# An encoder layer's output projection with two sets of places for its weights, the first half of its norm formed in the projection's own pass, and up products of two units around the last tile

## The chip, the core and the metric

The kernel runs on one core of one Trainium2 chip. TensorE multiplies matrices, VectorE and ScalarE work element by element, GpSimd (POOL) here mostly issues DMAs, and SyncE (SP) issues most of the others. The metric is the device time in microseconds (us) from launch to end; the time before is the median of three runs.

## The reference

One layer of a streaming encoder, for 1024 prompt frames and 64 sample frames of width 1024:

```python
merged = sigmoid(ga) * ya + sigmoid(gb) * yb
x = x + merged @ w_out                      # output projection, 1024 x 1024
n = x * rsqrt(mean(x * x) + 1e-6) * g_ffn
x = x + (silu(n @ w_ff1) * (n @ w_ff3)) @ w_ff2      # 1024 -> 2816 -> 1024
y = x * rsqrt(mean(x * x) + 1e-6) * g_final
```

What comes ahead of `merged` (a norm, one large input projection, a gated convolution, banded attention with its caches) is not touched. All is computed in float32.

## The kernel before

**Products of float32.** `split` writes a tensor as a high half (a ScalarE copy, CAST in the rows) and a low half (a VectorE subtraction of that copy). A product of two such tensors is three TensorE products: high x high, high x low, low x high. So nearly every operand costs one ScalarE and one VectorE operation before TensorE may use it, and the low half waits for the high half.

**Order.** The code is written straight down; a scheduler then fixes the order on each engine, and each engine works strictly through its own list. Pools (`tile_pool`) hold a number of places for each tag, and a new tile waits until the last user of its place is done.

**The merge** (`mgp`, names `ga`, `gb`, `ya`, `yb`) makes `merged` in eight rounds of 128 channels, each in three slices of the frames. It leaves it split, with channels on the partitions: `mg`, four tiles by channel half and frame half, and `ms` for the 64 sample frames. Its last product is on `yb`.

**Output projection.** Nine tiles of frames: 0 to 7 are prompt frames, tile 8 the sample frames. The result's 1024 columns are made in two passes of 512, in the order `ORDER` = 8, 0, 4, 1, 5, 2, 6, 3, 7. `wo_half(hf)` loads the weights of a pass (`wor`, two DMAs of 1 MB) and splits them into eight pairs `woh`, `wol` in a pool with eight places for each, so the second pass takes the places of the first. `token_product` issues 24 products for a prompt tile, 16 for tile 8 (`wo`); `residual` adds `x` on VectorE (for tile 8 after a ScalarE copy `fold`); the result goes to DRAM (`x1_d`).

**Second pass and norm.** `second(i)` loads the tile's first half back, adds the second half's result, forms the sum of squares over 1024 columns on ScalarE (line 891), the factor by `rstd_of` (square root on ScalarE, small VectorE rows, lines 228 to 234) and the normalised row `xg` by one VectorE operation over 1024 columns (line 893). `turned(i, xg)` transposes `xg` with eight TensorE operations into `xt`. For tiles 0 to 3 `first_half` splits `xt` into `mg` (reused as operands) and copies it to `sums`; for tiles 4 to 7, `second_half` forms sums and differences with the tile's partner in `sums` and splits them into `tt` 6, 7, 5 and the other `mg`.

**Up projection.** Frames and channels are halved, and each 2 x 2 block product is made with seven products, the steps `STEPS` = 1, 2, 6, 7, 5, 4, 3. A `Unit` is 256 columns of `w_ff1` (a0, a1, ...) or `w_ff3` (b0, b1, ...); the order is a0, b0, a1, b1 and so on. `prep(step)` splits the unit's weights (`wha`, `wla` for a, `whb`, `wlb` for b) from its raw load (`rawa`, `rawb`). Steps 1, 6, 5, 3 add up in PSUM tile A, 2 in B, 7 and 4 in D, so `Aa<-mg` is step 1 of a0, `Ba<-mg` step 2, `Aa<-tt` step 6 or 5, `Ab<-mg`, `Bb<-mg` steps 1 and 2 of b0. The first two steps read only `mg` of the first frame half. `run(unit, done, ahead, between)` issues all seven and prepares the next unit; for a0, `rest_of_x` is called after step 2 and turns the last tile (7):

```python
    def rest_of_x(si):
        ...
        if si == 1:
            turned(*last)
            wp_stack.close()
            hp = ctx.enter_context(tc.tile_pool(name="hp", bufs=2, reuse_waits="tile"))
            for st in range(2, len(STEPS)):
                unit.prep(st)
```

The down projection follows and is not touched.

Of the kernel before, what the change touches and what calls it, by code (L numbers as in the profile page):

```python
# [79 lines left out]
def encoder_kernel(ctx: ExitStack, tc: tile.TileContext, ins, outs):  # L80
# [717 lines left out]
    tt = {p: tpool.tile([P, 2, 4, HT], F32R, tag=f"o{p}", name=f"tt{p}") for p in (6, 7, 5)}  # L798
# [9 lines left out]

    def wo_half(hf):
        r = []  # L810
        for kq in range(2):
            raw = rpool.tile([P, 4, 512], F32, tag="raw", name=f"wor{hf}_{kq}")
            nc.sync.dma_start(
                raw,
                ins["w_out"][0][kq * 512 : (kq + 1) * 512, hf * 512 : (hf + 1) * 512].rearrange(
                    "(k p) n -> p k n", p=P
                ),
            )
            for k in range(4):
                hi = ws.tile([P, 512], F32R, tag="wh", name=f"woh{hf}_{kq}_{k}")  # L820
                lo = ws.tile([P, 512], F32R, tag="wl", name=f"wol{hf}_{kq}_{k}")
                split(hi, lo, raw[:, k])
                r.append((hi, lo))
        return r
# [602 lines left out]
```

## Time and profile before

| | us |
|---|---|
| three runs: median (lowest, highest) | 1553.8 (1553.78, 1555.74) |
| profiled execution, span from first to last instruction | 1555.5 |
| TensorE busy | 1511.3 |
| first pass of the projection, from the merge's last product on | 52.35 |
| second pass | 54.69 |
| from there to the end of step 2 of b0 | 44.69 |

For the profiled execution no time of its own stands beside its span; the highest of the runs is 0.2 above it. Rows read: start, duration, engine, line, operation, result<-operands, partitions x elements; in square brackets the idle time of the engine before it and what ended that. In the table by stage PEclk is the granted TensorE clock as a share of full speed. Matmuls overlap, so the distance of their starts, not their duration, is their price.

### The profile page before, as it was taken

Reading aid. Unit: us, or ns where it says so; the run is one execution under the profiler, and the core shown is the slowest. Engines: PE = TensorE matmul, PEld = TensorE weight load, DVE = VectorE, ACT = ScalarE, POOL = GpSimd, SP = SyncE. Lnnn points to the kernel's source line nnn. Section 1 sums busy time; section 2 is a strip of 40 time slices with the busy share of each in tenths; the row PEclk is TensorE's granted clock in tenths of the full one; section 3 lists DMA queues with packets and bytes.
Section 4 is the critical chain, followed back from the end, with each engine's and each line's share of the span. In section 5 each row is a group of like instructions: output and inputs, shape, how many; then the busy total and the mean of one; then the engine's idle time right before and its main releaser. Section 6 shows DMA issues by size and latency. Waiting matters only on the chain.

```text
span 1555.5 us, 24418 instructions
## 1 busy us (share of the span) xinstructions
PE 1511.3 (97%) x9407; PEld 1419.1 (91%) x9407; DVE 930.3 (60%) x1877; ACT 622.9 (40%) x1234; POOL 77.5 (5%) x146
## 2 busy tenths in 40 slices
PE   7998999999999999999997999999999999999997
PEld 6888999999999999998886999999999998788886
DVE  7524665555553435664388666666666667757577
ACT  7423454444442132442255444444444444512123
POOL 0110000000000000000100100000101111000000
PEclk9999999999999999999997999999999999999999
DMA  8688785444421323554331443334434338777685
GB/s 280 199 235 232 185 253 145 136 136 127 134 86 41 55 72 42 157 163 154 128 125 50 144 147 126 123 124 143 153 139 153 140 138 295 246 234 240 210 264 202
DMA packets 168661, 247.18 MB, mean 159 GB/s; under 512 B 17025, under 2 KB 117265, under 8 KB 168545
## 3 DMA queue, kind: packets, MB, share of 16 engines
q1 hardware_dynamic: 152400, 191.47, 40.6%
q0 software_dynamic: 14992, 52.05, 8.9%
q10 hardware_dynamic: 1152, 2.10, 0.4%
q8 instruction: 74, 1.21, 0.3%
q14 instruction: 43, 0.34, 0.1%
HBM read 161.91 MB, written 85.23 MB: 159 GB/s over the span
## 4 chain that ended last, share of the span: by engine, by line
PE 60%; issue 29%; DMA 4%; POOL 3%; DVE 3%; ACT 1%; SPq 0%; POOLq 0%; ACTq 0%; DVEq 0%
PE A L1349 7%; PE p L183 6%; PE p L184 6%; PE p L185 6%; PE D L1349 3%; POOL h_d L1100 2%; PE B L1349 2%; PE t L589 2%; PE pv L614 2%; PE Ab L1033 1%; PE ys L1237 1%; PE Aa L1033 1%; PE pvv L414 1%; PE pvv L412 1%; PE s L559 1%
## 5 line engine op out<-in xcount | busy, mean ns | idle before, releaser
L183 PE MATMUL p<-xn,whi 128*128 128x384 f32 (+1 forms) x576 | 193.2, 336 | 0.0
L184 PE MATMUL p<-xn,whi 128*128 128x384 f32 (+1 forms) x576 | 189.8, 330 | 0.0
L185 PE MATMUL p<-xn,wlo 128*128 128x384 f32 (+1 forms) x576 | 189.8, 329 | 0.0
L1349 PE MATMUL A<-ring,ht 128*128 128x512 f32 x528 | 127.7, 396 | 3.9 <-ACT acc L1359 3.8
L1349 PEld LDWEIGHTS A<-ring,ht 128*128 128x128 f32 x528 | 99.6, 190 | 27.2 <-ACT acc L1359 5.0
L183 PEld LDWEIGHTS p<-xn,whi 128*128 128x128 f32 x576 | 109.1, 189 | 1.4 <-DVE kst L131 0.3
L184 PEld LDWEIGHTS p<-xn,whi 128*128 128x128 f32 x576 | 109.2, 190 | 0.1
L185 PEld LDWEIGHTS p<-xn,wlo 128*128 128x128 f32 x576 | 108.9, 189 | 0.0
L522 DVE CUSTOM_DVE_ANT_0 p<-s,bias 128x640 f32<-128x640 f32 (+5 forms) x72 | 47.8, 664 | 98.2 <-PE s L560 98.1
L130 ACT CAST ring<-w2r 128x512 fp32r<-128x512 f32 (+1 forms) x78 | 43.6, 588 | 104.4 <-PE A L1349 50.8
L130 ACT CAST hq<-sa 128x512 fp32r<-128x512 f32 x77 | 47.7, 619 | 92.0 <-DVE sa L1112 58.1
L130 ACT CAST whi<-raw 128x1024 fp32r<-128x1024 f32 x44 | 46.0, 1050 | 92.5 <-PE ch L184 42.6
L131 DVE TENSOR_TENSOR hq<-sa,hq 128x512 fp32r<-128x512 f32 x77 | 53.1, 690 | 38.6 <-ACT hq L130 38.5
L131 DVE TENSOR_TENSOR wlo<-raw,whi 128x1024 fp32r<-128x1024 f32 x44 | 53.7, 1221 | 24.5 <-ACT whi L130 24.4
L1033 PE MATMUL Aa<-mg,wha 128*128 128x272 f32 x352 | 61.0, 295 | 3.9 <-ACT mg L130 3.2
L131 DVE TENSOR_TENSOR wla<-rawa,wha 128x512 fp32r<-128x512 f32 x55 | 37.8, 688 | 44.0 <-ACT wha L130 44.0
L1349 PE MATMUL D<-ring,ht 128*128 128x512 f32 x264 | 63.5, 392 | 0.0
L1100 POOL DMA_DIRECT2D h_d<-hq x77 | 41.0, 533 | 431.2 <-DVE hs L131 213.6
L1033 PE MATMUL Aa<-tt,wha 128*128 128x272 f32 x352 | 59.7, 291 | 2.2 <-ACT tt L130 2.2
L1349 PEld LDWEIGHTS D<-ring,ht 128*128 128x128 f32 x264 | 49.9, 189 | 11.1
L1033 PE MATMUL Ab<-mg,whb 128*128 128x272 f32 x352 | 58.3, 288 | 0.0
L1033 PE MATMUL Ab<-tt,whb 128*128 128x272 f32 x352 | 58.2, 287 | 0.0
(308 smaller groups left out, 3898.3 us busy)
## 6 DMA issues: line engine op xcount, KB each, us to landing
h_d<-hq POOLq DMA_DIRECT2D x77, 512.0 KB, 3.4
ht<-h_d SPq DMA_DIRECT2D x154, 256.0 KB, 3.5
raw<-in_w_in SPq DMA_DIRECT2D x18, 1024.0 KB, 5.7
rawa<-in_w_ff SPq DMA_DIRECT2D x11, 1024.0 KB, 5.7
rawb<-in_w_ff SPq DMA_DIRECT2D x11, 1024.0 KB, 5.4
w2r<-in_w_ff SPq DMA_DIRECT2D x11, 1024.0 KB, 6.0
qd<-q_d SPq DMA_DIRECT2D x32, 272.0 KB, 4.3
x<-in_x_prompt SPq DMA_DIRECT2D x8, 512.0 KB, 3.9
```

Source lines behind the costliest of these rows:

```text
L130: act.copy(hi, src)
L131: vec.tensor_tensor(lo, src, hi.bitcast(F32), op=ALU.subtract)
L183: mm(out, a, p, start=k == 0, stop=False)
L184: mm(out, a, q, start=False, stop=False)
L185: mm(out, b, p, start=False, stop=k == kt - 1)
L412: mm(pv[:n], a, wvh[:, k, :], start=k == 0, stop=False)
L522: vec.tensor_tensor_reduce(out=s if len(ps.shape) == 2 else s.rearrange("p (a b) -> p a b", a=2), in0=ps, in1=bias if len(ps.shape) == 2 e ...
L589: nc.tensor.transpose(tp[:, i * P : (i + 1) * P], s[:, i * P : (i + 1) * P], ident)
L614: mm(pv[:, :, lo:hi], v[:, kb, :], pt[:, :, kb - base, lo:hi], start=i == 0, stop=i == len(blocks) - 1,)
L1033: mm(t[:, j, :HN], x[:, k, :], moving(p, l, k, j * HN, HN), start=p in (1, 2, 7) and k == 0 and n == 0, stop=k == 3 and n == 2, skip_group ...
L1100: nc.gpsimd.dma_start(h_d[p, c - 1], hq.rearrange("p i l t -> p (i l t)").bitcast(F32))
L1349: mm(t, ht[k][:, j, x], w[:, l], start=p in (1, 2, 7) and k == 0 and n == 0, stop=k == len(ks) - 1 and n == 2, skip_group_check=p in (6, 5 ...
```

## The change

The first pass gets its own places for its weights: `wo_hi` (a pool on the side) is copied during the merge's last rounds, `wo_lo` is formed after the merge in the space that `tt` 7 takes later; the second pass's weights are split during the first pass. The first pass runs in the order 0 to 8 and forms, for each tile, the first half of the sum of squares (`more`) and the first half times the gain row, which goes to DRAM (`y0_d`) and comes back as the first half of `xg` in pass two. There ScalarE scales the first half and VectorE the second. `norm_factor` is moved up, and its factor of -2 is met by a gain row scaled by -0.5. `first_half` copies in two parts, and `sums` has four slots for five. Units a0 and b0 are started by hand: steps 1 and 2 of a0, the last tile's transposes (in PSUM places of their own), steps 1 and 2 of b0, and then the rest of a0. The weight sum `s1` moves from preparation step 2 to 3.

```diff
+    def wo_load(hf):
+        ...
+            raw = rpool.tile([P, 4, 512], F32, tag="raw", name=f"wor{hf}_{kq}")
+            nc.sync.dma_start(raw, ...)
     with tc.tile_pool(name="mgp", bufs=3, reuse_waits="tile") as mp:
...
+                if m == 7:
+                    wo_raw = wo_load(0)
+                    wo_hi = t6pool.tile([P, 8, 512], F32R, tag="o6", name="wo_hi")
+                    for k in range(8):
+                        act.copy(wo_hi[:, k], wo_raw[k // 4][:, k % 4])
...
+        act.activation(gb_row, gb_row, AF.Copy, scale=-0.5)
+        for k in range(8):
+            vec.tensor_tensor(wo_lo[:, k], wo_raw[k // 4][:, k % 4], wo_hi[:, k].bitcast(F32), op=ALU.subtract)
+        w2_raw = wo_load(1)
-        for i in ORDER:
+        for i in range(9):
...
-            token_product(ps, i, mg_rows(i), KD, lambda k: w[k])
+            token_product(ps, i, mg_rows(i), KD, lambda k: (wo_hi[:, k], wo_lo[:, k]))
             residual(i, ps, xt, 512, f"o0_{i}")
             nc.gpsimd.dma_start(x1_d[t0 : t0 + n, :512], xt[:n])
+            act.activation(sq[:n, :512], xt[:n], AF.Square, accum_out=ssq0[:n, i : i + 1])
+            vec.tensor_scalar(more[:n, i : i + 1], ssq0[:n, i : i + 1], 1.0 / D, EPS, op0=ALU.mult, op1=ALU.add)
+            y0 = wp.tile([P, D], F32, tag="xg", name=f"y0_{i}")[:, :512]
+            vec.tensor_tensor(y0[:n], xt[:n], gb_row[:n, :512], op=ALU.mult)
+            nc.gpsimd.dma_start(y0_d[t0 : t0 + n], y0[:n])
+            if i < 8:
+                w2_prep(i)
         def second(i):
-            xt = wp.tile([P, D], F32, tag="x1", name=f"x1_{i}")
-            nc.sync.dma_start(xt[:n, 512:], x_rows(i)[:, 512:])
-            nc.sync.dma_start(xt[:n, :512], x1_d[t0 : t0 + n, :512])
+            nc.sync.dma_start(xg[:n, :512], y0_d[t0 : t0 + n])
+            nc.sync.dma_start(xt[:n], x_rows(i)[:, 512:])
...
-            act.activation(xg[:n], xt[:n], AF.Square, accum_out=ssq[:n])
-            r = rstd_of(wp, ssq[:n], n, f"f{i}")
-            vec.scalar_tensor_tensor(xg[:n], xt[:n], r[:n], gb_row[:n], op0=ALU.mult, op1=ALU.mult)
+            act.activation(sq[:n, :512], xt[:n], AF.Square, accum_out=ssq[:n])
+            r = norm_factor(wp, ssq[:n], n, f"f{i}", more[:, i : i + 1])
+            act.activation(xg[:n, :512], xg[:n, :512], AF.Copy, scale=r[:n])
+            vec.scalar_tensor_tensor(xg[:n, 512:], xt[:n], r[:n], gb_row[:n, 512:], op0=ALU.mult, op1=ALU.mult)
...
+    sa_step(0)
+    sa_step(1)
+    turned(*last)
+    wp_stack.close()
+    hp = ctx.enter_context(tc.tile_pool(name="hp", bufs=2, reuse_waits="tile"))
+    for si in range(2, len(STEPS)):
+        ua.prep(si)
+    sb_step(0)
+    sb_step(1)
+    for si in range(2, len(STEPS)):
+        sa_step(si)
+        ub.prep(si)
```

Line numbers shift: 891, 893, 903, 927, 1033 and 1100 become 929, 932, 949, 973, 1080 and 1131. Names carry numbers of their own in the order below (`wo0_8`: pass one, tile 8; the last number only counts tiles).

TensorE at the start of the first pass, before:

```order
L836 MATMUL wo0_8_7464<-woh0_0_0_7428,ms_6436 128x512 [waits DVE_49,Activation_49]
L832 MATMUL wo0_0_7488<-woh0_0_0_7428,mg00_6429 128x512 [waits DVE_49]
L837 MATMUL wo0_8_7464<-wol0_0_0_7429,ms_6436 128x512 [waits DVE_49]
L836 MATMUL wo0_8_7464<-woh0_0_1_7432,ms_6436 128x512 [waits Activation_49]
L833 MATMUL wo0_0_7488<-wol0_0_0_7429,mg00_6429 128x512
L837 MATMUL wo0_8_7464<-wol0_0_1_7433,ms_6436 128x512 [waits DVE_49]
L836 MATMUL wo0_8_7464<-woh0_0_2_7436,ms_6436 128x512 [waits Activation_49]
L834 MATMUL wo0_0_7488<-woh0_0_0_7428,mg00_6429 128x512
```

and now:

```order
L837 MATMUL wo0_0_7459<-wo_hi_7295,mg00_6430 128x512 [waits DVE_49]
L837 MATMUL wo0_1_7497<-wo_hi_7295,mg00_6430 128x512 [waits DVE_49]
L838 MATMUL wo0_0_7459<-wo_lo_7435,mg00_6430 128x512 [waits DVE_49]
L839 MATMUL wo0_0_7459<-wo_hi_7295,mg00_6430 128x512
L837 MATMUL wo0_0_7459<-wo_hi_7295,mg00_6430 128x512
L838 MATMUL wo0_1_7497<-wo_lo_7435,mg00_6430 128x512
L839 MATMUL wo0_1_7497<-wo_hi_7295,mg00_6430 128x512
L838 MATMUL wo0_0_7459<-wo_lo_7435,mg00_6430 128x512 [waits DVE_49]
```

Tile 0 stands first where tile 8 stood, no high half is waited for, and only the low halves (`wo_lo`, on VectorE) are.

VectorE around the last tiles, the rows from the residual of tile 3 to its normalised second half, now (before there were 23 rows from the residual to `xg_3`, with all of tile 6's norm among them):

```order
L855 TENSOR_TENSOR x_3_8229<-wo_3_8231,x_3_8229 128x512
L973 TENSOR_TENSOR sums_8220<-xt_6_8272,sums_8220 128x512
L869 TENSOR_SCALAR nvf_8260<-ssq_3_8258,more 128x1
L973 TENSOR_TENSOR sums_8220<-xt_6_8272,sums_8220 128x512
L871 RECIPROCAL nyf_8262<-nsf_8261 128x1
L132 TENSOR_TENSOR wla_1_8362<-rawa_8357,wha_1_8361 128x512
L872 SCALAR_TENSOR_TENSOR nzf_8263<-nyf_8262,nvf_8260 128x1
L973 TENSOR_TENSOR sums_8220<-sums_8220 128x512
L873 SCALAR_TENSOR_TENSOR nrf_8264<-nzf_8263,nyf_8262 128x1
L132 TENSOR_TENSOR tt_7792<-sums_8220,tt_7792 128x4x128
L932 SCALAR_TENSOR_TENSOR xg_3_8227<-x_3_8229,nrf_8264,gb_row 128x512
```

These are the rows that the transposes of tile 3 wait for. VectorE further down, the last rows up to the low half of `mg` from tile 3's transposes, which step 1 of a0 waits for, before:

```order
L927 TENSOR_TENSOR sums_8185<-sums_8185 128x512 x2
L131 TENSOR_TENSOR mg_6432<-xt_6_8237,mg_6432 128x4x128
L131 TENSOR_TENSOR tt_7419<-sums_8185,tt_7419 128x4x128
L131 TENSOR_TENSOR mg_6431<-sums_8185,mg_6431 128x4x128
L850 TENSOR_TENSOR x_7_8260<-wo_7_8263,x_7_8260 128x512
L131 TENSOR_TENSOR wla_6_8423<-sf,wha_6_8422 128x512
L131 TENSOR_TENSOR wla_7_8428<-rawa_8322,wha_7_8427 128x512
L131 TENSOR_TENSOR wla_5_8432<-sf,wha_5_8431 128x512
L228 TENSOR_SCALAR v_f_8293<-ssq_7_8291 128x1
L131 TENSOR_TENSOR wla_4_8436<-rawa_8322,wha_4_8435 128x512
L230 RECIPROCAL y_f_8295<-s_f_8294 128x1
L131 TENSOR_TENSOR mg_6429<-xt_3_8306,mg_6429 128x4x128
```

and now:

```order
L132 TENSOR_TENSOR tt_7790<-sums_8220,tt_7790 128x4x128
L973 TENSOR_TENSOR sums_8220<-sums_8220 128x512
L132 TENSOR_TENSOR mg_6433<-xt_6_8272,mg_6433 128x4x128
L855 TENSOR_TENSOR x_7_8297<-wo_7_8299,x_7_8297 128x512
L132 TENSOR_TENSOR mg_6432<-sums_8220,mg_6432 128x4x128
L132 TENSOR_TENSOR wla_2_8366<-rawa_8357,wha_2_8365 128x512
L869 TENSOR_SCALAR nvf_8328<-ssq_7_8326,more 128x1
L132 TENSOR_TENSOR wlb_1_8370<-rawb_8359,whb_1_8369 128x512
L871 RECIPROCAL nyf_8330<-nsf_8329 128x1
L132 TENSOR_TENSOR wlb_2_8374<-rawb_8359,whb_2_8373 128x512
L872 SCALAR_TENSOR_TENSOR nzf_8331<-nyf_8330,nvf_8328 128x1
L132 TENSOR_TENSOR mg_6430<-xt_3_8340,mg_6430 128x4x128
```

From tile 3's residual to that low half VectorE has 37 operations before (23 over 512 or more columns a partition) and 24 now (17 of them so).

TensorE around the transposes of the last tile, before:

```order
L1033 MATMUL Ba0_8366<-mg10_6430,wha0_2_8328 128x272 x4
L1033 MATMUL Ba0_8366<-mg10_6430,wla0_2_8329 128x272 x2
L903 MATMUL xt2_7_8394<-ident_69,xg2_7_8290 128x128 x8
L1033 MATMUL Aa0_8335<-tt6_7418,wha0_6_8422 128x272
L1033 MATMUL Da0_8480<-tt7_7419,wha0_7_8427 128x272
L1033 MATMUL Aa0_8335<-tt6_7418,wha0_6_8422 128x272 x2
L1033 MATMUL Da0_8480<-tt7_7419,wha0_7_8427 128x272 x2
L1033 MATMUL Aa0_8335<-tt6_7418,wha0_6_8422 128x272
L1033 MATMUL Aa0_8335<-tt6_7418,wla0_6_8423 128x272 x2
```

and now, with what follows up to the first product that reads `tt`:

```order
L1080 MATMUL Ba0_8404<-mg10_6431,wha0_2_8365 128x272 x4
L1080 MATMUL Ba0_8404<-mg10_6431,wla0_2_8366 128x272 x2
L949 MATMUL xt2_7_0_8432<-ident_69,xg2_7_8295 128x128 x4
L949 MATMUL xt2_7_1_8433<-ident_69,xg2_7_8295 128x128 x4
L1080 MATMUL Ab0_8484<-mg00_6430,whb0_1_8369 128x272 x4
L1080 MATMUL Ab0_8484<-mg00_6430,wlb0_1_8370 128x272 x2
...
L1080 MATMUL Bb0_8511<-mg10_6431,whb0_2_8373 128x272 x4
L1080 MATMUL Bb0_8511<-mg10_6431,wlb0_2_8374 128x272 x2
...
L1080 MATMUL Aa0_8377<-tt6_7792,wha0_6_8462 128x272 x4
```

Two steps of b0, 48 products, stand between the transposes and the first product on `tt` 6, where there was nothing. In pass two each tile's transposes now stand directly ahead of a product group; before they stood up to 18 products into one.

More of the change, by code (lines that the diff above doesn't have):

```diff
@@ L763, in encoder_kernel @@
     ms = mspool.tile([P, KD, 2, TS], F32R, tag="ms", name="ms")
+    t6pool = ctx.enter_context(tc.tile_pool(name="t6pool", bufs=1, reuse_waits="tile", side="right"))
+    wo_raw = []
+    def wo_load(hf):
+        r = []
+        for kq in range(2):
+            raw = rpool.tile([P, 4, 512], F32, tag="raw", name=f"wor{hf}_{kq}")
+            nc.sync.dma_start(
+                raw,
+                ins["w_out"][0][kq * 512 : (kq + 1) * 512, hf * 512 : (hf + 1) * 512].rearrange(
+                    "(k p) n -> p k n", p=P
+                ),
+            )
+            r.append(raw)
+        return r
     with tc.tile_pool(name="mgp", bufs=3, reuse_waits="tile") as mp:
@@ L796, in encoder_kernel @@
     hp0 = ctx.enter_context(tc.tile_pool(name="hp0", bufs=1, reuse_waits="tile"))
[L798 removed]
+    wo_lo = tpool.tile([P, 8, 512], F32R, tag="o7", name="wo_lo")
     ax = mg.t
@@ L807, in column @@
         return i * P if i < 4 else HT + (i - 4) * P
[L809 to L824, printed above, removed]
     def token_product(ps, i, x, kt, w, first=True, last=True):
@@ L898, in turned @@
             n = TT[i][1]
-            pt = bank2("A", f"xt2_{i}").rearrange("p a (b t) -> p a b t", t=P)
+            if i == ORDER[-1]:
+                pt = [
+                    psA.tile([P, 512], F32, tag="mm", name=f"xt2_{i}_{hf}").rearrange("p (b t) -> p b t", t=P)
+                    for hf in range(2)
+                ]
+            else:
+                two = bank2("A", f"xt2_{i}").rearrange("p a (b t) -> p a b t", t=P)
+                pt = [two[:, 0], two[:, 1]]
             for hf in range(2):
@@ L1009, in prep, with runner @@
                 self.plain(3, a12)
-    def run(unit, done, ahead, between=None):
+    def runner(unit, done):
         nm = unit.nm
@@ L1022, in shot, with step @@
             snap[key] = s
-        for si, p in enumerate(STEPS):
+        def step(si):
+            p = STEPS[si]
             key = {1: "A", 6: "A", 5: "A", 3: "A", 2: "B", 7: "D", 4: "D"}[p]
@@ L1052, in run @@
                 done(0, 1, src, None)
-            if between:
-                between(si)
-            for u in ahead:
-                u.prep(si)
-    nxt_unit = Unit(ins["w_ff1"][0][:, : 2 * P], "a0")
-    nxt_unit.prep(0)
-    nxt_unit.prep(1)
-    hp = None
-    def rest_of_x(si):
-        nonlocal hp
-        if si == 1:
-            turned(*last)
-            wp_stack.close()
-            hp = ctx.enter_context(tc.tile_pool(name="hp", bufs=2, reuse_waits="tile"))
-            for st in range(2, len(STEPS)):
-                unit.prep(st)
+        return step
+    hp = None
     names = [(l, p) for p in range(NF // 2) for l in "ab"]
@@ L1256, in encoder_kernel @@
             refill()
-        run(unit, (gate_done if l == "a" else hidden_done)(p), ahead, rest_of_x if n == 0 else None)
+        step = sb_step if n == 1 else step_of(n, unit)
+        for si in range(len(STEPS)):
+            if n > 1 or si > 1:
+                step(si)
+            for u in ahead:
+                u.prep(si)
+        unit = nxt_unit
     up_stack.close()
```

93 lines of the change are left out of this document (58 added, 35 removed).

## Prediction

> **What bounds the kernel now.** First the page's busy shares: TensorE works 97% of the span, so only a stretch in which it stands still or runs at a lower clock can give time back.
>
> ```profile
> PE 1511.3 (97%) x9407; PEld 1419.1 (91%) x9407; DVE 930.3 (60%) x1877; ACT 622.9 (40%) x1234; POOL 77.5 (5%) x146
> PEclk9999999999999999999997999999999999999999
> ```
>
> The one dip of the granted clock inside the span is in the slice from 817 to 856, the end of the output projection. So second, a table by stage: the projection's first pass, its second pass, the join to the up products (to the end of the second step of unit b0), and what follows.
>
> ```profile
> core 0: us, PE busy (x) PEld busy (x) DVE busy (x) ACT busy (x) POOL busy (x), PEclk, DMA share, GB/s
> 713.70:766.05 52.35, 50.14 (x208) 40.23 (x209) 16.65 (x27) 9.53 (x18) 4.37 (x8) 0.97 0.44 146
> 766.05:820.74 54.69, 54.69 (x266) 44.43 (x264) 43.60 (x108) 30.53 (x63) 4.88 (x9) 1.00 0.42 144
> 820.74:865.43 44.69, 35.61 (x232) 34.03 (x232) 31.43 (x56) 20.17 (x35) 0.54 (x1) 0.81 0.18 58
> 865.43:905.00 39.57, 38.93 (x312) 38.71 (x311) 26.68 (x45) 17.27 (x33) 4.29 (x8) 1.00 0.40 146
> ```
>
> Pass two and the stage after it are full; the loss is at the start of pass one and in the join. Third, TensorE's timeline there.
>
> ```profile
> 713.39 0.31 PE L185 MATMUL yb<-ob,wlo 128*128 128x320 f32 x1
> 715.91 0.50 PE L836 MATMUL wo<-woh,ms 128*128 128x512 f32 x1 [2.21 <-ACT woh L130]
> ...
> 760.49 0.40 PE L832 MATMUL wo<-woh,mg 128*128 128x512 f32 x1
> 766.05 0.39 PE L836 MATMUL wo<-woh,ms 128*128 128x512 f32 x1
> 769.69 0.39 PE L832 MATMUL wo<-woh,mg 128*128 128x512 f32 x1
> ...
> 820.50 0.29 PE L1033 MATMUL Ba<-mg,wha 128*128 128x272 f32 x1
> 823.55 1.94 PE L903 MATMUL xt<-ident,xg 128*128 128x128 f32 x8 [2.77 <-DVE xg L893]
> 829.69 0.82 PE L1033 MATMUL Aa<-mg,wha 128*128 128x272 f32 x2 [3.16 <-ACT mg L130]
> 830.79 0.59 PE L1033 MATMUL Aa<-mg,wha 128*128 128x272 f32 x1 [0.28 <-DVE mg L131]
> ...
> 842.51 0.52 PE L1033 MATMUL Aa<-tt,wha 128*128 128x272 f32 x2 [2.18 <-ACT tt L130]
> 843.24 0.82 PE L1033 MATMUL Da<-tt,wha 128*128 128x272 f32 x2 [0.21 <-ACT tt L130]
> ...
> 862.42 0.66 PE L1033 MATMUL Bb<-mg,whb 128*128 128x272 f32 x4
> 865.43 0.66 PE L1033 MATMUL Ab<-tt,whb 128*128 128x272 f32 x4
> ```
>
> A tile of 24 products takes 766.05 - 760.49 = 5.56 us (0.232 each), the sample tile's 16 take 3.64, a step of an up unit 865.43 - 862.42 = 3.01. Pass one is worth 8 x 5.56 + 3.64 = 48.1 and takes 52.35: 4.2 lost. The join is worth nine steps (27.1) and two groups of transposes (0.94 each, below), 29.0, and takes 44.69: 15.7 lost. Each gap drags a slow clock behind it, but not always:
>
> ```profile
> 716.95:720.40 3.45, 3.45 (x10) 2.64 (x9) 3.45 (x7) 2.54 (x5) 0.00 (x0) 0.51 0.87 226
> 822.85:836.20 13.35, 8.73 (x35) 7.76 (x36) 12.45 (x26) 5.77 (x11) 0.54 (x1) 0.50 0.21 67
> 843.40:846.80 3.40, 3.40 (x16) 3.35 (x17) 2.83 (x5) 0.89 (x2) 0.00 (x0) 0.53 0.00 0
> 1104.30:1108.00 3.70, 3.70 (x31) 3.70 (x31) 2.89 (x5) 2.21 (x5) 0.53 (x1) 1.00 0.54 217
> ...
> 1103.14 0.78 PE L1033 MATMUL Da<-tt,wha 128*128 128x272 f32 x4 [2.19 <-DVE sa L1087]
> 890.21 0.78 PE L1033 MATMUL Da<-tt,wha 128*128 128x272 f32 x4 [0.64 <-DVE sa L1087]
> ```
>
> Gaps of 2.21 and 2.18 us were followed by some 3.4 us at half clock, one of 2.19 by none.
>
> **The change, part by part.** VectorE and ScalarE rows that carry the terms:
>
> ```profile
> 713.74 0.49 DVE L781 TENSOR_TENSOR gb<-yb,gb 128x320 f32<-128x320 f32 x1 [0.94 <-PE yb L185]
> 715.88 4.91 DVE L131 TENSOR_TENSOR wol<-wor,woh 128x512 fp32r<-128x512 f32 x8
> 715.24 4.25 ACT L130 CAST woh<-wor 128x512 fp32r<-128x512 f32 x8
> 814.05 0.69 DVE L850 TENSOR_TENSOR x<-wo,x 128x512 f32<-128x512 f32 x1 [1.36 <-PE wo L834]
> 822.12 1.28 DVE L893 SCALAR_TENSOR_TENSOR xg<-x,r_f,gb_row 128x1024 f32<-128x1024 f32 x1
> 830.07 0.67 DVE L131 TENSOR_TENSOR mg<-xt,mg 128x512 fp32r<-128x512 f32 x1
> L893 DVE SCALAR_TENSOR_TENSOR xg<-x,r_f,gb_row 128x1024 f32<-128x1024 f32 x6 | 7.7, 1283 | 0.2
> L891 ACT ACTIVATE xg<-x 128x1024 f32<-128x1024 f32 x7 | 7.4, 1059 | 2.1 <-DVE x L850 2.1
> ```
>
> In a row, a 128x512 operation takes (4.91 - 0.69) / 7 = 0.60 on VectorE and (4.25 - 0.62) / 7 = 0.52 on ScalarE.
>
> *Start of pass one.* The eight copies of the weights' high halves move into the merge: 4.25 us on ScalarE, spread over its last 40 us, where it is not the limit (row below). The two loads keep their places in SP's queue. Tile 0 comes first, whose merged rows are done a third of a round early. The low halves stay behind the last merge product: the first follows the multiply of 713.74, starts near 714.2, ends near 714.9. TensorE has two products before that (to 714.2), so 0.7 us of gap remains. The other seven low halves come every 0.60, with about 1.1 for the merge's last slice between, and end near 720.0; the 27 products that TensorE has by then need 27 x 0.232 = 6.3 us, to 721.2, so it sets the pace. Gain 4.2 - 0.7 = 3.5. Ends: 1.8 if the slow clock comes after all (3.45 us at half cost 1.7), 4.2 if nothing is left. I take 3.4; the gap of 0.64 at 890 kept the full clock.
>
> ```profile
> 680.00:714.00 34.00, 33.70 (x206) 33.43 (x204) 19.49 (x42) 12.95 (x31) 0.00 (x0) 1.00 0.37 112
> x_d<-xr POOLq DMA_DIRECT2D x8, 256.0 KB, 2.6
> x<-x_d SPq DMA_DIRECT2D x8, 256.0 KB, 3.0
> ```
>
> *Rest of pass one.* Per tile VectorE gains a product with the gain row (0.69), one split (0.69) and a small row, beside the residual (0.69): 2.2 of 5.56 us. ScalarE gains a square over 512 (estimate 0.6, half of 1059 ns and a fixed part) and a copy (0.62). Cost 0; the cover is the tile's 5.56 us. The second weights no longer wait for free places, which cost nothing before either (766.05 follows without a gap).
>
> *Round trip of y0.* POOL issues nine more stores; SP's nine reloads of x1 become nine of y0. The tight one is the sample tile, last in pass one and first in pass two. After its last product: copy, two adds and the product with the gain row, 0.2 + 0.6 + 3 x 0.69 = 2.9; the store (behind another, 0.5) lands 2.6 later, the reload 3.0 after that, a scale of 0.6: 9.6 us. TensorE needs it after 3.64 + 5.56 + 10 x 0.232 = 11.5. Cost 0, slack 1.9; if the slack is gone, the price is the excess, once, since SP holds the next reloads only that long.
>
> *Pass two.* Its 54.69 are 48.1 of products and seven groups of transposes, 0.94 each. Both stay. But before, a tile's transposes stand as late as 18 products into the next tile but one; now each group stands ahead of the next product, so a tile's chain from residual to normalised row must fit into 0.94 + 5.56 = 6.5 us. For tile 3, VectorE has seven large rows and four small ones up to its last: 7 x 0.60 + 4 x 0.15 = 4.8, or 5.2 with the ScalarE steps waited for. For tile 1, the fullest, it has eight large and four small, 5.4, and some 0.5 where a low half waits for ScalarE's copy: 5.9. It fits by 0.6. Cost 0; ends -0.8 (split waits inside the old groups) and three such tiles 1.5 late, +4.5.
>
> *Join, first gap.* Before, TensorE ran freely at 830.79, 10.05 after pass two. What ends last is the low half of tile 3's first block (830.07). From that tile's residual to there VectorE works through 23 large rows, two of them 1.28 long, and 14 small: 23 x 0.60 + 2 x 0.6 + 14 x 0.1 = 16.4, measured 830.74 - 814.05 = 16.7. Now it is 17 large and 7 small: 17 x 0.60 + 7 x 0.13 = 11.1, with 0.4 of waits 11.5. The residual starts 0.2 after its product and that ends 6.5 before pass two does, so the end is 5.2 to 5.4 after pass two. Gain 10.05 - 5.4 = 4.7. Ends 3 and 6. The slow clock after it I leave as it was (830.79 to 836.20).
>
> *Join, second gap.* After tile 7's transposes TensorE now has two steps of unit b0, 6.0 us. VectorE needs eight large rows for the first sum that the next step reads: 4.8, with waits 5.3. So the gap of 2.18 + 0.21 goes, and the half clock behind it (3.40 x 0.47 = 1.6): gain 4.0. If that cover failed, what is late next is the second sum, 0.6 behind.
>
> Sum: 3.4 + 0 + 4.7 + 4.0 = 12.1 us, which makes the span 1543.4 from 1555.5. The span is 1.7 above the median of the runs (1553.8), 0.2 under the highest; I take the 12.1 from the median: 1541.7.
>
> The remaining first gap is about 3 us, with a product or two in it. The Trainium skill, page "TensorE: Matmul & The Clock Gate", section "Why this matters for your kernels", warns only of idle gaps above about 3 us. By that rule the restart would keep the full clock, and the sum would be that of rival 3 below. The row of 2.21 with clock 0.51 behind it does not agree with the rule, the row of 2.19 with 1.00 behind it does.
>
> **The rivals.** (1) *Transposes late.* Three of the tiles whose chain shares VectorE with a second-half tile miss the 6.5 us by 1.5: for it speaks the margin of 0.6, against it that VectorE's work per pair falls. 12.1 - 4.5 = 7.6: 1546.2. (2) *No gain at the start*: the low halves alone keep TensorE waiting, and the clock drops as at 716.95; 8.7 remains: 1545.1. (3) *No slow clock in the join*: the 5.4 us at half clock from 830.79 to 836.20 cost 2.7, so 12.1 + 2.7 = 14.8: 1539.0. The gap at 1103.14 speaks for it, the clock from 823 to 836 against. (4) *Slower*: the transposes ahead of the products turn every tile's chain into a wait. If the chain stays as long as tile 3's was (814.05 to 823.40, 9.4 us), seven tiles pay 9.4 - 6.5 = 2.9 each, 20.3 in all: 12.1 - 20.3 = 8.2 slower, 1562.0. It decides from a chain of 6.5 + 12.1 / 7 = 8.2 us on. Against it: the shorter list of rows above. (5) *Nothing*: a chain of about 8.2 us, or the join's gain lost to later waits on the same VectorE queue; the full stage after 865.43 speaks against it.
>
> **How the numbers follow.** Forecast 0.61 (own range 1539.5 to 1544.5), rival 1 0.13, 2 0.08, 3 0.07, 4 0.06, 5 0.05. Faster by over 0.2% (3.1 us, about what a measurement of this kernel can tell from no change): 0.61 + 0.13 + 0.08 + 0.07 = 0.89; within it 0.05; slower 0.06. The range takes the first four cases: low 1553.8 - (4.2 + 4.7 + 4.0 + 2.7) - 1 for a shorter first gap, about 1537.0; high 1546.2 and the 1.7 of a slow clock at the start, about 1548.0. What lies outside is 4 and 5 and a little more.
>
> **What would show it.** In the new trace: a gap under 1 us ahead of the first projection product and a clock of 1.00 behind it (pass one near 49 us); pass two still near 54.7 with no wait ahead of transposes; the first up product running freely some 5.4 us after pass two; no gap after tile 7's transposes; that join near 36 us. The forecast is wrong if transposes wait tile by tile, or if the first gap stays near 10 us because ScalarE's copy of tile 3 comes later than VectorE's list says.

## The result and the profile after

The changed kernel takes 1543.5 us (median of 4 runs, 1542.41 to 1545.24), the kernel before 1553.8 (4 runs), ratio 0.9931 with a 95% interval of 0.9917 to 0.9945. The forecast was 1541.7, range 1537.0 to 1548.0. The changed kernel's profiled execution took 1543.16 us, its span 1541.4. Its page, busy shares and granted clock:

```profile
PE 1503.1 (98%) x9407; PEld 1413.3 (92%) x9407; DVE 930.4 (60%) x1877; ACT 630.5 (41%) x1267; POOL 82.3 (5%) x155
PEclk9999999999999999999999999999999999999999
```

TensorE's busy time fell by 8.2 us with the same 9407 instructions: part of the gain is clock, and the dip is gone from the row. The table by stage, cut as before (columns as in its header):

```profile
core 0: us, PE busy (x) PEld busy (x) DVE busy (x) ACT busy (x) POOL busy (x), PEclk, DMA share, GB/s
714.26:763.55 49.29, 48.57 (x210) 39.05 (x209) 23.20 (x44) 11.65 (x27) 8.69 (x16) 1.00 0.66 230
763.55:817.92 54.37, 54.37 (x265) 44.54 (x264) 42.09 (x98) 33.45 (x76) 5.41 (x10) 1.00 0.37 118
817.92:852.32 34.40, 31.14 (x233) 30.53 (x232) 29.15 (x52) 19.67 (x38) 1.08 (x2) 0.95 0.25 84
```

Pass one is 3.1 shorter, pass two as long as it was, the join 10.3 shorter. TensorE's timeline at the same places:

```profile
714.11 0.31 PE L186 MATMUL yb<-ob,wlo 128*128 128x320 f32 x1
714.26 0.62 PE L837 MATMUL wo<-wo_hi,mg 128*128 128x512 f32 x2
715.60 0.50 PE L838 MATMUL wo<-wo_lo,mg 128*128 128x512 f32 x1 [0.72 <-DVE wo_lo L888]
...
817.69 0.40 PE L839 MATMUL wo<-woh,mg 128*128 128x512 f32 x1
817.93 1.04 PE L949 MATMUL xt<-ident,xg 128*128 128x128 f32 x8
818.72 0.37 PE L1080 MATMUL Ba<-mg,wha 128*128 128x272 f32 x1
819.36 0.36 PE L1080 MATMUL Aa<-mg,wha 128*128 128x272 f32 x1 [0.28 <-DVE mg L132]
822.03 0.52 PE L1080 MATMUL Aa<-mg,wha 128*128 128x272 f32 x2 [2.31 <-ACT mg L131]
823.23 0.40 PE L1080 MATMUL Aa<-mg,wha 128*128 128x272 f32 x1 [0.68 <-DVE mg L132]
...
830.39 1.03 PE L949 MATMUL xt<-ident,xg 128*128 128x128 f32 x8
831.18 0.75 PE L1080 MATMUL Ab<-mg,whb 128*128 128x272 f32 x4
```

The start's gap is 0.72 instead of 2.21. The transposes of tile 3 (817.93) follow pass two without a wait; 2.77 stood there before. What is left is three waits, 0.28 + 2.31 + 0.68 = 3.3 us, up to the first product that runs freely, 823.23, 5.31 after pass two. Behind tile 7's transposes (830.39) b0's first step follows at once, where 2.18 + 0.21 stood.

Below, the stages of each experiment are cut the same way on TensorE's timeline: pass one from the merge's end, pass two, the join up to the 217th up product (nine steps of 24 before it), and the rest of the span.

| kernel | median us | ratio (95%) | pass one | pass two | join | rest |
|---|---|---|---|---|---|---|
| before, profile shown | 1553.8 | | 52.5 | 54.4 | 44.9 | 690.1 |
| before again | 1553.3 | 0.999 (0.9974 to 1.0006) | 52.4 | 54.4 | 44.6 | 686.1 |
| after | 1543.5 | 0.9931 (0.9917 to 0.9945) | 49.3 | 54.4 | 34.4 | 689.0 |
| after again | 1543.8 | 0.994 (0.9922 to 0.9957) | 49.3 | 54.4 | 34.4 | 687.2 |
| early high halves undone | 1544.5 | 0.9934 (0.992 to 0.9949) | 49.8 | 54.4 | 34.2 | 690.0 |
| tile 8 first | 1544.8 | 0.9937 (0.9921 to 0.9952) | 49.3 | 54.4 | 35.0 | 688.7 |
| two sets of places undone | 1552.1 | 0.9988 (0.9976 to 0.9999) | 50.9 | 59.0 | 35.6 | 691.2 |
| norm division undone | 1543.4 | 0.9922 (0.9905 to 0.9939) | 49.3 | 54.3 | 34.2 | 685.9 |
| division and factor undone | 1546.0 | 0.9951 (0.9936 to 0.9966) | 49.3 | 54.4 | 38.1 | 687.9 |
| before with the factor | 1551.9 | 0.9991 (0.9982 to 1.0) | 52.5 | 54.4 | 42.2 | 686.9 |
| steps of b0 undone | 1549.4 | 0.9965 (0.9953 to 0.9977) | 49.3 | 54.4 | 37.9 | 691.7 |
| column halves | 1539.5 | 0.991 (0.9897 to 0.9923) | 49.3 | 54.4 | 30.2 | 690.6 |
| column halves, no division | 1541.0 | 0.9909 (0.9895 to 0.9923) | 49.3 | 54.4 | 31.2 | 689.6 |
| y0 stored by ScalarE's queue | 1541.2 | 0.9916 (0.9901 to 0.9932) | 49.3 | 54.4 | 35.1 | 687.0 |

Each ratio is against the kernel before in the same batch on the same chip. Single executions of one kernel lie up to some 10 us apart, so one profile's rest is worth about +-2 us; the stages repeat to 0.1 where the clock does.

### The profile page after: what moved, and what is told of

Read it like the earlier page. It is cut to its first block, busy times and chain, and to the rows that moved or that the text cites. A ratio compares the mean times of both kernels' runs of the same rounds, so it can differ in the third digit from the quotient of the medians.

```text
span 1541.4 us, 24484 instructions
## 1 busy us (share of the span) xinstructions
PE 1503.1 (98%) x9407; PEld 1413.3 (92%) x9407; DVE 930.4 (60%) x1877; ACT 630.5 (41%) x1267; POOL 82.3 (5%) x155
## 4 chain that ended last, share of the span: by engine, by line
PE 66%; issue 22%; DVE 4%; DMA 4%; POOL 2%; ACT 1%; SPq 1%; POOLq 0%; ACTq 0%; DVEq 0%
PE A L1401 6%; PE p L184 6%; PE p L185 6%; PE p L186 6%; PE Ab L1080 3%; PE Aa L1080 3%; PE D L1401 3%; PE Da L1080 2%; PE B L1401 2%; PE t L590 2%; PE pv L615 2%; PE Db L1080 2%; DMA h_d<-hq 1%; POOL h_d L1131 1%; PE pvv L415 1%
## 5 line engine op out<-in xcount | busy, mean ns | idle before, releaser
L131 ACT CAST ring<-w2r 128x512 fp32r<-128x512 f32 (+1 forms) x78 | 43.4, 588 | 103.7 <-PE A L1401 50.9
L1401 PEld LDWEIGHTS D<-ring,ht 128*128 128x128 f32 x264 | 49.5, 188 | 11.5 <-ACT acc L1411 0.4
L316 ACT COPY gst<-p 128x384 f32<-128x384 f32 (+1 forms) x48 | 22.1, 460 | 89.3 <-PE p L186 72.2
```

The lines of the kernel that those rows point to most:

```text
L131: act.copy(hi, src)
L316: act.copy(st[:, :n], ps)
L1401: mm(t, ht[k][:, j, x], w[:, l], start=p in (1, 2, 7) and k == 0 and n == 0, stop=k == len(ks) - 1 and n == 2, skip_group_check=p in (6, 5 ...
```

## The experiments

### The two kernels once more

The changed kernel and the kernel before, run again with nothing edited.

> The changed kernel once more, nothing edited. If the profile of it is typical, its time is 1543.5 us again (ratio 0.992 to 0.994), the gap ahead of the first projection product is 0.7 us, the gaps after tile 3's transposes add up to 3.3 us, and some 2.8 us of half clock follow. If the short stretch of half clock was luck, that stretch is 5 us or more this time and the join up to 2 us longer.

> The kernel before once more, nothing edited, for its profile. If the first profile is typical in the stages (pass one 52.5 us, pass two 54.4, join 45.4), they come out within 1 us of that, and the two stretches of half clock in the down projection (which cost 3.4 us there) may be absent, which leaves a span near 1552. If the first profile's join was unusually long, the join is 42 us or less this time.

After: the same stages to 0.01 us, 1543.8, and again one stretch of 3.41 at half clock in the join. Before, its table by stage:

```profile
715.47:767.82 52.35, 50.14 (x211) 40.16 (x209) 16.65 (x27) 9.54 (x18) 4.37 (x8) 0.97 0.44 146
767.82:822.24 54.42, 54.42 (x265) 44.44 (x264) 43.33 (x108) 30.26 (x62) 4.88 (x9) 1.00 0.42 143
822.24:866.87 44.63, 34.65 (x233) 33.00 (x232) 31.69 (x56) 20.45 (x36) 0.54 (x1) 0.85 0.18 59
```

The stages are those of the first profile. By the traces they gain 151.9 - 138.1 = 13.8 or 151.4 - 138.1 = 13.3; the medians show 10.3 (11.2 in the batch in which the changed kernel was repeated). So by the medians some 2 to 3 us come back outside the three stages (the intervals of the two ratios allow gains from 6.7 to 12.9). The rests of the profiles do not show it as they stand: 690.1 and 686.1 before, 689.0 and 687.2 after, 688.1 on average for both. But the first profile before has two windows at half clock behind the join (1324.47 to 1327.88 and 1338.12 to 1341.53), about 1.7 us each, and the other three have none. Without them the kernel before has 686.4 on average, and the changed kernel is 1.7 longer.

### The start: early high halves, and tile 0 first

Without the early copies, the high halves in a place that comes free only after the merge:

```diff
-                    wo_hi = t6pool.tile([P, 8, 512], F32R, tag="o6", name="wo_hi")
-                    for k in range(8):
-                        act.copy(wo_hi[:, k], wo_raw[k // 4][:, k % 4])
...
+    wo_hi = tpool.tile([P, 8, 512], F32R, tag="o5", name="wo_hi")
...
         for k in range(8):
+            act.copy(wo_hi[:, k], wo_raw[k // 4][:, k % 4])
             vec.tensor_tensor(wo_lo[:, k], ...)
```

> Only the start is undone: the high halves of the first weights get a place that comes free after the merge, so that ScalarE forms them there, as before the change. Theory (the prediction's term): the gap ahead of the first product is about 2 us again, half clock follows for some 3.4 us, pass one takes 52.3 instead of 49.3 us, and the time is 3.1 to 3.4 us above that of the changed kernel, about 1546.8. Rival (no gain at the start): the low halves alone set the pace, and the time is within 1 us of the changed kernel's.

Its timeline, ScalarE's row and then TensorE's:

```profile
711.98 1.66 ACT L886 CAST wo_hi<-wor 128x512 fp32r<-128x512 f32 x3 [1.72 <-PE yb L186]
...
712.65 0.72 PE L835 MATMUL wo<-wo_hi,mg 128*128 128x512 f32 x2 [0.71 <-ACT wo_hi L886]
713.65 0.51 PE L836 MATMUL wo<-wo_lo,mg 128*128 128x512 f32 x1 [0.28 <-DVE wo_lo L887]
```

The gaps are 0.71 + 0.28 and no half clock follows: pass one 49.8 instead of 49.3. My theory, that the early copies carry the start, fell. ScalarE had been idle for 1.72 when the place came free, so its copy took only 0.7 of TensorE's time. (The first pass keeps its own places here.)

The other candidate is the order. The changed kernel with the sample tile first again in pass one:

```diff
-        for i in range(9):
+        for q, i in enumerate(ORDER):
...
-            if i < 8:
-                w2_prep(i)
+            if q < 8:
+                w2_prep(q)
```

> The changed kernel, but pass one runs in the old order of the tiles, the sample tile (8) first, which needs the last merged rows at once; the high halves are still formed in the merge. Theory: what opened the old gap was the wait for the last merged rows on ScalarE and VectorE; tile 8 first brings part of it back, a gap of 1.5 to 2 us, and pass one takes 50.5 to 52 us for 49.3. Rival: with the high halves there in time the order is free, the gap stays at 0.7 and pass one at 49.3 us.

Pass one 49.27, its gap 0.72, unchanged: with the high halves early, the order is free. With two sets of places, either part alone keeps the gap at 1 us or less. With neither, and one set:

### Two sets of weight places undone

`wo_half` as before the change: one set of eight places for both passes, split after the merge, tile 8 first; all else as changed.

```diff
+    def wo_half(hf):
+        ...
+                split(hi, lo, raw[:, k])
...
+        w = wo_half(0)
-        for i in range(9):
+        for i in ORDER:
-            if i < 8:
-                w2_prep(i)
+        w2 = wo_half(1)
```

> Only the places of the weights and the tile order of pass one are undone: one set of places as before, both halves of the first weights formed after the merge, tile 8 first, the second weights split when the first are done; the norm's division, its factor and the two early steps of b0 stay. Theory (ScalarE's order, not the place alone, made the old gap): ScalarE again has the casts of the merge's last rows ahead of the first high half, the gap is 2.2 us, it fills most of one 3.41 us window of the clock, half clock follows for 3.4 us, pass one takes 52.3 instead of 49.3, and the time is 3 us above the changed kernel's (about 1546.7). Rival: as in the run with the start undone by a place alone, a gap of 1 us without half clock and a time within 1 us of the changed kernel's.

Both expectations were short: 1552.1 us, about 8.3 above the changed kernel. Its timeline, with rows of ScalarE, TensorE and VectorE:

```profile
714.98 0.40 ACT L131 CAST mg<-ga 128x256 fp32r<-128x256 f32 x1 [2.77 <-DVE ga L799]
...
716.10 0.50 PE L852 MATMUL wo<-woh,ms 128*128 128x512 f32 x1 [2.21 <-ACT woh L131]
...
772.36 0.69 DVE L1035 TENSOR_TENSOR sf<-rawa 128x512 f32<-128x512 f32 x1 [5.00 <-DMA rawa<-in_w_ff]
...
779.49 0.71 PE L950 MATMUL xt<-ident,xg 64*128 64x64 f32 x8 [3.12 <-ACT xg L932]
```

The start's gap is back, 2.21, because the high half for tile 8 stands behind the casts of the merge's last slice. The larger loss is one that neither theory named: VectorE waited 5.00 us for a0's raw weights, whose load is issued at 764.94 here and at 728.29 in the changed kernel, with a weight sum queued ahead of the sample tile's residual. The sample tile's row came late, TensorE stood 3.12 us before its transposes and had a half clock after them: pass two 59.0 instead of 54.4. So what is undone here, sets, early halves and tile order together, is worth 1.6 at the start, where this time no half clock followed the gap. In pass two it keeps a0's preparation, in the order of this kernel, from blocking the norm. That cover the prediction had not looked for: it wrote that the wait for free places "cost nothing before either", which was right only for the old order.

### The norm: the division by halves, and the factor

First the division alone: the first half is again reloaded from `x1_d`, and square and scaling run over 1024 columns in pass two; the factor's form (`norm_factor`) stays.

```diff
-            act.activation(sq[:n, :512], xt[:n], AF.Square, accum_out=ssq0[:n, i : i + 1])
-            ...
-            nc.gpsimd.dma_start(y0_d[t0 : t0 + n], y0[:n])
...
+            act.activation(xg[:n], xt[:n], AF.Square, accum_out=ssq[:n])
+            r = norm_factor(wp, ssq[:n], n, f"f{i}")
+            vec.scalar_tensor_tensor(xg[:n], xt[:n], r[:n], gb_row[:n], op0=ALU.mult, op1=ALU.mult)
```

> Only the norm's division is undone: pass one forms neither the sum of squares nor the product with the gain row, nothing goes out to DRAM and back, and pass two squares and scales 1024 columns at once as before; the start and the two early steps of unit b0 stay. Theory (the prediction's term for the first gap): VectorE's list gets longer again, the first step of a0 runs freely about 10 us after pass two instead of 5.3, and the time rises by 4 to 5 us, to about 1548. Rival: the list was shortened by the order of the rows rather than by the division; counted in the order of this kernel there are 15 large and 7 small rows from tile 3's residual to the low half that is waited for, so that point stays near 5.3 and the time within 1.5 us of the changed kernel's.

The join is 34.2, no longer than with the division, and the time 1543.4. The theory fell: forming the first half in pass one gains nothing here. Then the factor as well (`rstd_of` with its six small VectorE rows and the unscaled gain row), and by itself in the kernel before:

```diff
-        act.activation(gb_row, gb_row, AF.Copy, scale=-0.5)
-            r = norm_factor(wp, ssq[:n], n, f"f{i}")
+            r = rstd_of(wp, ssq[:n], n, f"f{i}")
```

and, on the kernel before:

```diff
+        act.activation(gb_row, gb_row, AF.Copy, scale=-0.5)
-            r = rstd_of(wp, ssq[:n], n, f"f{i}")
+            r = norm_factor(wp, ssq[:n], n, f"f{i}")
```

> The norm's division is undone as before, and with it the norm's factor: the six small VectorE rows of the old form instead of four. Theory: the factor is what brought each tile's chain under its cover; in the order of this kernel tile 6's transposes stand 18 products late again (only the first product ahead of them in the kernel with the division alone undone), step 1 of a0 runs freely near 10 us after pass two, and the time is 5 to 8 us above the changed kernel's, about 1549 to 1551. Rival: the lateness comes from the order of tiles or the weights' splitting, and the time stays within 1.5 us of the changed kernel's.

> The kernel before with one edit: the norm's factor in four small VectorE rows for six, and the gain row scaled by -0.5 for it. Theory: this alone takes the first gap of the join from 10 us to about 5.5 after pass two and leaves the start's gap (2.2 us) and the gap after tile 7's transposes (2.2 us); the time falls by 5 to 7 us from the kernel before, to 1547 to 1549. Rival: without the division nothing moves, and the time is that of the kernel before within 1.5 us.

TensorE's timeline with both undone:

```profile
821.24 1.06 PE L942 MATMUL xt<-ident,xg 128*128 128x128 f32 x8 [3.38 <-DVE xg L925]
826.01 1.32 PE L1073 MATMUL Aa<-mg,wha 128*128 128x272 f32 x3 [1.80 <-ACT mg L131]
```

and in the kernel before with the factor:

```profile
821.87 1.06 PE L914 MATMUL xt<-ident,xg 128*128 128x128 f32 x8 [0.87 <-DVE xg L904]
826.84 0.77 PE L1044 MATMUL Aa<-mg,wha 128*128 128x272 f32 x2 [2.80 <-ACT mg L130]
828.04 0.59 PE L1044 MATMUL Aa<-mg,wha 128*128 128x272 f32 x1 [0.44 <-DVE mg L131]
```

Where TensorE runs freely after pass two: 5.24 with the division undone, 8.43 with the factor undone too; 10.31 before, 7.33 before with the factor. So the factor is worth 3.0 to 3.2 us of the 5.0 by which the first gap shrank, from either side. Two small rows fewer for a tile are far from 3 us by themselves. What they change is the order of VectorE's list. In the kernel before, tile 6's `xg` comes behind tile 3's residual (814.05); with the factor it comes ahead of it. VectorE's rows, before and then with the factor:

```profile
816.99 1.28 DVE L893 SCALAR_TENSOR_TENSOR xg<-x,r_f,gb_row 128x1024 f32<-128x1024 f32 x1
```

```profile
813.76 1.28 DVE L904 SCALAR_TENSOR_TENSOR xg<-x,nrf,gb_row 128x1024 f32<-128x1024 f32 x1
...
815.55 0.68 DVE L850 TENSOR_TENSOR x<-wo,x 128x512 f32<-128x512 f32 x1
```

From that residual to the low half that step 1 waits for, VectorE has 37 rows before (23 of them large) and 25 with the factor (18 large); 32 (20 large) with both undone and 22 (16 large) with the division alone undone. Both expectations had too large a size. In time the factor alone is not clear of noise (ratio 0.9991, up to 1.0); the join shows it, 42.2 for 44.6 to 44.9. The other 2 us belong to the rest of the change together; no run parts them.

### The two steps of b0

All of a0 first, as before the change, the last tile's transposes again in PSUM tile A.

```diff
     sa_step(0)
+    ub.prep(0)
     sa_step(1)
     turned(*last)
...
-    sb_step(0)
-    sb_step(1)
+    ub.prep(1)
```

> Only the start of unit b0 is undone: after tile 7's transposes comes step 3 of a0 (which reads what tile 7 gives), b0 follows after all of a0, and the transposes of tile 7 take their old kind of PSUM place. Theory (the prediction's term for the second gap): a gap of about 2.2 us (2.4 with the small one behind it) and some 3.4 us of half clock stand behind tile 7's transposes again, and the time rises by 4.0 us, to about 1547.5. Rival: VectorE's queue is shorter by now, the sums of tile 7 come in time, and the time rises by less than 1.5 us.

The median is 5.6 above the changed kernel's in the same batch, 3.9 by the ratios (0.9965 - 0.994 of 1555); the join is 3.5 longer. Its TensorE timeline behind tile 7's transposes:

```profile
832.52 0.52 PE L1074 MATMUL Aa<-tt,wha 128*128 128x272 f32 x2 [2.30 <-ACT tt L131]
833.67 0.40 PE L1074 MATMUL Aa<-tt,wha 128*128 128x272 f32 x1 [0.63 <-DVE tt L132]
```

The gap is back, and the price is near the 4.0 of the theory, but from other terms: the two gaps are 2.9 us for 2.4, and no half clock follows here, as the last section shows.

### What fills the first gap

The longest wait left in the first gap of the changed kernel, 2.31, ends with ScalarE's queue; the last one, 0.68, with VectorE's list. Rows of ScalarE, and then the low half on VectorE:

```profile
819.17 0.61 ACT L131 CAST wha<-rawa 128x512 fp32r<-128x512 f32 x1
819.70 0.61 ACT L131 CAST wha<-sf 128x512 fp32r<-128x512 f32 x1
820.22 0.63 ACT L929 ACTIVATE sq<-x 128x512 f32<-128x512 f32 x1
...
820.84 0.56 ACT L966 COPY sums<-xt 128x512 f32<-128x512 f32 x1
821.41 0.57 ACT L131 CAST mg<-xt 128x512 fp32r<-128x512 f32 x1
...
822.49 0.68 DVE L132 TENSOR_TENSOR mg<-xt,mg 128x512 fp32r<-128x512 f32 x1
```

Tile 3's transposes are done by 819.0 (817.93 + 1.04); its copy comes at 820.84 and its cast at 821.41, behind two weight casts and tile 7's square. VectorE works without a pause from 812.55 to the end of its row, 823.17. Steps 1 and 2 of a0 make two column halves (j, 272 frames each), and only the second reads what is made from tile 3. So the first column halves of both steps go first, 24 products that need none of it:

```diff
-        def step(si):
+        def step(si, cols=(0, 1)):
...
-                    for j in range(2):
+                    for j in cols:
...
+            if 1 not in cols:
+                return
...
-    sa_step(0)
-    sa_step(1)
+    sa_step(0, (0,))
+    sa_step(1, (0,))
+    sa_step(0, (1,))
+    sa_step(1, (1,))
```

> The changed kernel with one more edit: steps 1 and 2 of a0 each run their first half of the columns (tiles 0 to 2 alone) before the second half, so that TensorE has 24 products (3.0 us) after pass two that need nothing of tile 3. Theory: the first gap of 3.3 us shrinks to about 1 us, no window of the clock is idle for half its length, no half clock follows, and the time falls by 3.5 to 4.5 us from the changed kernel, to about 1539.5. Rival: the low halves of the second step's weights, or tile 7's chain, end last then, and the gap only moves: within 1.5 us of the changed kernel.

Its TensorE timeline in the join, and its table by stage:

```profile
816.84 1.04 PE L949 MATMUL xt<-ident,xg 128*128 128x128 f32 x8
...
822.14 0.39 PE L1080 MATMUL Aa<-mg,wha 128*128 128x272 f32 x1 [0.51 <-DVE mg L132]
```

```profile
816.83:847.07 30.24, 29.58 (x233) 28.99 (x232) 28.88 (x52) 19.75 (x37) 1.08 (x2) 1.00 0.28 95
```

Gaps of 0.15 and 0.51 are left and the clock stays at 1.00: the join is 4.2 shorter, the median 1539.5, 4.0 below the changed kernel's (3.3 by the ratios, whose intervals just touch). This version has the lowest median of all. Is it better without the division, which gained nothing above?

> The two best edits so far together: the changed kernel with its norm's division undone and with the first half of the columns of steps 1 and 2 of a0 run first. Theory: the division gains nothing once the factor is short, and its nine stores cost the wait near 1130 us; so the join stays near 30 us, that wait goes, and the time is 1 to 2 us below the run with the column halves alone, about 1538. Rival: without the division tile 7's chain or tile 3's ends late once the column halves have taken the slack, the join is 32 us or more, and the time is above 1540.

The edit is that of the division above, on the kernel with the column halves. It is not: 1541.0, join 31.2, with 1.22 of waiting for `wla`. Its interval and that of the column halves nearly coincide, so the two are equal within what was measured.

### What comes back behind the join

TensorE's waits between 860 and 1300, on the sums `sa`, add up to 5.0 and 3.5 us in the two profiles of the changed kernel, and to 4.1 and 2.4 in those of the kernel before. One near 1130 is new. All engines' timeline around it, changed kernel:

```profile
1122.65 0.69 DVE L132 TENSOR_TENSOR hq<-sa,hq 128x512 fp32r<-128x512 f32 x1 [0.69 <-ACT hq L131]
...
1126.17 0.54 POOL L1131 DMA_DIRECT2D h_d<-hq  x1 [5.35 <-DVE sa L1134]
...
1131.17 0.62 ACT L131 CAST hq<-sa 128x512 fp32r<-128x512 f32 x1 [3.65 <-DMA h_d<-hq]
...
1133.21 0.78 PE L1080 MATMUL Da<-tt,wha 128*128 128x272 f32 x4 [1.69 <-DVE sa L1118]
```

A store of `hq` whose data was ready at 1123.34 is issued by POOL at 1126.17, 2.83 us late; POOL had been idle for 5.35, and the release in its brackets is not that of the data. It is the third of its unit's seven, and the sixth takes its place: ScalarE waits 3.65 for it to land, VectorE's sum comes late, TensorE stands 1.69. Each of the fourteen profiles shows exactly one `hq` store that late, always the third of a unit: after 110 earlier DMAs by POOL where the nine `y0` stores are not POOL's (then at 1165 to 1182, where ScalarE waits 1.7 for it and TensorE not at all), after 111 where they are (at 1121 to 1135, where ScalarE waits 3.1 to 3.9 and TensorE 1.1 to 2.0). Why the store lands later in the earlier unit is not shown. To test the count, the nine stores are issued by ScalarE instead:

```diff
-            nc.gpsimd.dma_start(y0_d[t0 : t0 + n], y0[:n])
+            nc.scalar.dma_start(y0_d[t0 : t0 + n], y0[:n])
```

> The changed kernel, with the nine stores of the first half of the scaled rows issued by ScalarE's queue instead of POOL's. In every profile so far one store of POOL comes 2.83 us late, at the 111th DMA that POOL issues where there are nine more (there TensorE then waits 1.1 to 2.0 us in the up units near 1130 us) and at the 110th where there are not (there nobody waits). Theory: the count decides, so the late store moves back to the later place, the wait near 1130 us goes, and the time falls by 1 to 2 us to about 1542. Rival: that wait comes from the traffic or the order of the up units; it stays, and the time is within 0.5 us of the changed kernel's.

Its timeline of POOL's stores:

```profile
1123.42 0.53 POOL L1131 DMA_DIRECT2D h_d<-hq  x1 [2.82 <-DVE hq L132]
...
1167.93 0.54 POOL L1131 DMA_DIRECT2D h_d<-hq  x1 [5.32 <-DVE sa L1134]
```

The store at 1123.42 follows its data at once (the release in its brackets is `hq`). The late one is now that of 1167.93, whose data was ready at 1165.13. The wait near 1130 is gone, and the median is 1541.2, 2.3 below the changed kernel's. That the late store moves with the number of POOL's DMAs and takes the wait with it is shown by the traces; for the time alone the two intervals overlap. Over all fourteen profiles the rest is 689.8 on average in the seven with the late store at the earlier place and 687.6 in the other seven, some 2 us apart; with 1.7 taken off for each window at half clock behind the join it is 689.3 and 686.1, some 3 us apart. The wait itself is 1.1 to 2.0 of that; what makes up the remainder is not shown. In the profile with the column halves this wait, 1.91, has half clock behind it as well (1129.76 to 1133.17). The column halves with the nine stores on ScalarE's queue were not run. Why one store in about 110 is late is open.

## Why the prediction was right, and where it missed

- **Start of pass one.** Predicted 3.4 (gap 0.7, no slow clock, pass one near 49); the trace gives 3.1 to 3.2, gap 0.72, clock 1.00. Right in size. That it needs the early copies, as the step has it, is not borne out: with two sets of places the new order alone leaves 1.0 of gap and no slow clock, pass one 49.8.
- **Rest of pass one, round trip of y0 within the passes.** Predicted 0; pass one 49.3, no wait on `y0`. Right there.
- **Pass two.** Predicted 0, it is 54.4 in both, and transposes wait for nothing. The margin of 0.6 held.
- **First gap.** Predicted 5.2 to 5.4 after pass two; 5.31. The reason held too. The list of 24 rows from tile 3's residual was to take 11.5 us; it takes 823.17 - 811.67 = 11.50, without a pause from 812.55 on, and TensorE runs freely at 823.23. ScalarE's queue, which the step left out, ends the wait before (2.31 <-ACT mg), but not the last one (0.68 <-DVE mg). What made the list shorter was mainly the factor, which the step does not name: it puts tile 6's norm ahead of tile 3's residual. The halves formed in pass one did not shorten it: without them the end is 5.24.
- **Slow clock behind it, "as it was (830.79 to 836.20)".** Mis-sized: 5.4 us were predicted, one stretch of 3.41 was there. At half cost that is 1.0 us more gain; what else the join gained over the predicted 8.7 (0.5 to 0.8) is not parted.
- **Second gap.** Predicted 4.0 with its half clock. The gap is gone, and the kernel before has both terms in its rows: right. The undoing cost 3.5 in the join and 3.9 by the ratios, but as 2.9 of gaps without half clock; that the figures agree so closely is luck.
- **Sum.** Predicted 12.1; the three stages gained 13.3 to 13.8, the medians 10.3 to 11.2. **What failed is the step from the stages to the whole time**: nothing was counted behind the join, although the part on y0 had nine more stores on POOL. They were costed only up to where `y0` is read ("Cost 0, slack 1.9"). By the traces they move one late store, some 280 us behind the join, to a place where TensorE waits 1.1 to 2.0 us for it; by the medians that is about 2 us, which the intervals do not settle. This and the slow clock that was counted too long partly cancel, so that 1541.7 lies as near to 1543.5 as it does is in part luck.

Of the rivals, late transposes (1), no gain at the start (2), slower (4) and nothing (5) fell: pass two has no waits, and pass one is 49.3. Rival 3, no slow clock in the join, was partly right: it shrank. The Trainium skill's warning (page "TensorE: Matmul & The Clock Gate", section "Why this matters for your kernels"), gaps only above about 3 us, was quoted there; the 1.88 of idle time shown in the last section, followed by a half clock, goes against it again.

## What to carry to other kernels

Count the rows in the queues of both engines that feed TensorE, up to the one it waits for: that gave the first gap's size here, and a gap that stays can be filled with products that read nothing of the late tile (4 us here). When a change adds instructions to a queue, look through the whole remaining program for places where that queue's releases are tight, not only at the stage that was changed. Undo a change part by part before keeping it: of this one, the division of the norm gained nothing, the factor that came along with it 3 us of the first gap (by putting rows into another order), and the added places mattered most in a stage that the change was not about.
